# A decoder trunk on one core: the row scale moved behind the projections, gated attention in 128-row matmuls, and the first up-projection sums on VectorE

## The chip, the cores and the metric

The kernel runs on one core of a Trainium2 chip. The metric is the device time of one execution in microseconds, the median of several; lower is better. A core has five engines with queues of their own: PE (TensorE, matmuls and transposes; its weight loads are shown apart as PEld), DVE (VectorE), ACT (ScalarE), POOL (GpSimd) and SP (SyncE, here the queue that issues most transfers). Each engine works off its instructions in order and waits on semaphores of the others. Matmul results go to eight banks of PSUM.

## The reference, cut to what matters

One decoder layer on x of 1024 rows by 1024 columns, in float32:

```python
h = x * rsqrt(mean(x*x, -1) + 1e-6) * mix_norm
z = h @ w_in        # columns: gq 256, gk 256, gv 512, gr 512, glr 16, sq 512, sk 128, sv 128
log_a = log_sigmoid(glr @ w_alpha2 + b_alpha) / 16
o_gla = silu(gr) * rms_norm(gated_linear_attention(gq / 8, gk, gv, log_a))    # 4 heads of 64 / 128
o_swa = sliding_window_attention(rms_norm(sq), rms_norm(sk), sv, sinks)       # 8 heads of 64, window 128
x = x + concat([o_gla, o_swa]) @ w_out
u = causal_depthwise_conv3(rms_norm(x) @ w_up)      # 1024 -> 2 x 2816
a, b = split(u)
out = x + (silu(a) * b) @ w_down
```

## The kernel before, in words

Rows are worked in eight tiles of 128 (t = 0 to 7). A product that has to be near float32 is made of three fast passes: `split` (L90) stores an operand as a rounded part `hi` (a cast on ACT) and a remainder `lo` (a subtraction on POOL or DVE), and PE multiplies hi x hi, hi x lo and lo x hi. So one tile's projection of 1024 to 512 columns is 24 matmuls of 128x512 (`dense`, L279; `unit_q_part`, L643, for the first ones, named `dq`). The transposed, split rows are kept in `big`, the split weights in `qw`, `kw`, `vw`, `gw`, `rw` and `wow` by stage. Matmuls on plain float32 operands (the gated attention's and the small ones) aren't split.

The stages follow each other: the query projection `dq` with the first norm, the K and gate projection `dk`, the V projection `dv`, then `dg` (gated attention's q and k) and `dr` (its output gate) with both attentions between, the output projection `do` (two halves of columns), and the FFN, whose up and down products are made with seven instead of eight block products (operands such as A11, A12, S1 to S4 are blocks of w_up or sums of them). Before the first norm's transposes, `norm1_stat` squares a row tile on ACT, turns the sum into 1/sqrt on DVE and POOL (`rms_scale`, L156), and multiplies x by that and by `mix_norm` on DVE. `mix_norm` is spread over the partitions by a matmul with one row of ones (`mix`, L1003). Then PE transposes the tile (`n1pt`, L238), ACT and DVE split it into `big`. The x tiles take turns in three buffers.

In the sliding-window part K's tile and the 16 gate columns are transposed (`kpt`), and the gate's 17 rows (16 and one of ones) times `wa` give `za` (L368). In the gated part each tile has scores `ga` (L532, with 64 of the 128 partitions per head), `go` (L543, scores times values, and L546, queries times the running state `s_mid`) and the state's increment `cs` (L508).

The code lists steps with times in units of a tile (`at`), is sorted by them, and the framework's scheduler then sets each engine's order by a simulated timeline, so that instructions of several steps mix. Around the output projection the steps `up_operand` (L719) and `first_sums` (L713) prepare the first weights of the FFN: splits on ACT and POOL, sums on POOL. At the same time `norm2_stat` and `norm2_rows` (L183, L190) do the second norm: squares on ACT, `n2v` on DVE, the power `n2r` on POOL, two products `n2h` on DVE, and the transposes `n2pt` on PE. The last step, `last_row` (L973), makes eight row tiles of the last two chunks; each half of a tile is added on DVE and sent out by SP.

Of the kernel before, what the change touches and what calls it, by code (L numbers as in the profile page):

```python
# [9 lines left out]
F32 = mybir.dt.float32  # L10
# [7 lines left out]
P = 128  # L18
T = 1024
D = 1024  # L20
# [14 lines left out]
def hymba_layer_kernel(ctx, tc, x, mix_norm, w_in, w_alpha2, b_alpha, gla_norm,  # L35
# [31 lines left out]
    RAW_BUFS, K4, K2 = 3, 6, 4  # L67
# [51 lines left out]

    for h in range(8):  # L120
# [28 lines left out]

    def load_x(t, parts=1):  # L150
# [13 lines left out]

    def norm1_stat(t):
        xt = xts[t]
        junk = px.tile([P, D], F32, tag="junk", name=f"junk_{t}", bufs=1)
        ss = px.tile([P, 2], F32, tag="n1ss", name=f"n1ss_{t}", bufs=2)
        if t == 0:
            act.activation(junk[:, 0:512], xt[:, 0:512], AF.Square, accum_out=ss[:, 0:1])  # L170
            dve.tensor_tensor_reduce(junk[:, 512:], xt[:, 512:], xt[:, 512:], 1.0, ss[:, 0:1],
                                     ALU.mult, ALU.add, ss[:, 1:2])
        else:
            act.activation(junk, xt, AF.Square, accum_out=ss[:, 1:2])
        r = rms_scale(ss[:, 1:2], D, 1, f"n1{t}", px, "n1")
        for i, c in enumerate(halves):
            dve.scalar_tensor_tensor(xt[:, c], xt[:, c], r[:, 0:1], mixn[:, c] if t > 1 else mix_ps[i],
                                     op0=ALU.mult, op1=ALU.mult)

    def norm1_tr(t):  # L180
        norm_tr(t, xts.pop(t), "n1")
# [50 lines left out]

    def norm_tr(t, h, tag):
        for q in range(2):
            pt = bank(f"{tag}pt_{t}_{q}")
            for k in range(4):
                c = (q * 4 + k) * P
                pe.transpose(pt[:, k * P:(k + 1) * P], h[:, c:c + P], ident)  # L238
            ptv = pt.rearrange("p (k c) -> p k c", k=4)
            hi, lo = big[:, t, q * 4:q * 4 + 4, 0, :], big[:, t, q * 4:q * 4 + 4, 1, :]  # L240
            act.copy(hi, ptv)
            dve.tensor_sub(lo, ptv, hi.bitcast(F32))
# [10 lines left out]
    def raw_dma(name, c0, n, k2):  # L253
# [3 lines left out]
        if name == "k":  # L257
            sp.dma_start(rv[:, :, 0:256], rows[:, :, CSK:CSK + 256])
            sp.dma_start(rv[:, :, 256:272], rows[:, :, CG:CG + 16])
        else:  # L260
            sp.dma_start(rv, rows[:, :, c0:c0 + n])

# [35 lines left out]
    wa = gl.tile([17, 256], F32, name="wa")  # L298
    glan = gl.tile([P, 1], F32, name="glan")

    def load_small():
# [6 lines left out]
        sp.dma_start(wa[16:17, :], b_alpha)  # L308
        dve.tensor_mul(sinks_s, sinkb, islope)
# [5 lines left out]
    def head_rms(ps_ap, nh, name):  # L315
        sq = k2_tile(name + "sq")
        act.activation(sq[:, :nh * HD], ps_ap, AF.Square)
# [5 lines left out]
    def q_post(t, pb):  # L323
        r = head_rms(pb, 8, f"q{t}")
        rs = gl.tile([P, 8], F32, tag="rs", name=f"rs{t}", bufs=2)
        dve.tensor_mul(rs, r, qscale)
# [8 lines left out]
    def kvl_post(t, pb):  # L335
        r = head_rms(pb[:, 0:P], 2, f"k{t}")
        act.copy(vv[:, t, :], pb[:, P:2 * P])
        gn = gl.tile([P, 17], F32, tag="gn", name=f"gn{t}", bufs=4)
        pool.memset(gn[:, 16:17], 1.0)
        dve.tensor_copy(gn[:, 0:16], pb[:, 256:272])  # L340
# [7 lines left out]
    def kvl_tr(t):  # L348
# [12 lines left out]
        gt = gl.tile([17, P], F32, tag="gt", name=f"gt{t}", bufs=1)  # L361
        act.copy(gt, pt[0:17, P:2 * P])
# [86 lines left out]

    state = gl.tile([P, 2, P], F32, name="state")  # L450
    s_mid = [gl.tile([P, 2, 256], F32, name=f"s_mid{i}") for i in range(2)]
    asb = [gl.tile([P, 2, 256], F32, name="asb0")]
    for s in s_mid + asb:
        pool.memset(s, 0.0)
# [29 lines left out]
    def gla_qk(t, pb):  # L484
# [3 lines left out]
        dve.scalar_tensor_tensor(qk[:, 0:256], pb[:, 0:256], 0.125, ex[:, 0], op0=ALU.mult, op1=ALU.mult)  # L488
        dve.tensor_mul(qk[:, 256:512], pb[:, 256:512], ex[:, 1])
        if t < NT - 1:  # L490
            dve.tensor_mul(kd, pb[:, 256:512], ex[:, 2])
        gqk[t] = qk

    def gla_tr(t):
# [4 lines left out]
        qt = k2_tile(f"gqt{t}").rearrange("p (i c) -> p i c", i=4)  # L499
        act.copy(qt, pb.rearrange("p (i c) -> p i c", i=4))  # L500
        gqt[t] = qt
# [16 lines left out]
    def gla_mid(t):  # L518
        dc, sm = gdec[t], s_mid[t % 2]
        for h in range(4):  # L520
            pr, lo = h // 2, h % 2
            r = HALF[lo]
            act.activation(sm[r, pr, lo * P:(lo + 1) * P], state[r, pr], AF.Copy,
                           scale=dc[r, pr * 2:pr * 2 + 1])

    def gla_a(t):
        qt = gqt[t]
        for lo in range(2):
            pb = bank(f"ga{t}_{lo}")
            r = slice(lo * 64, (lo + 1) * 64)  # L530
            for pr in range(2):
                pe.matmul(pb[:, pr * P:(pr + 1) * P], lhsT=qt[r, 2 + pr, :], rhs=qt[r, pr, :],  # L532
                          start=True, stop=True)
            dve.copy_predicated(asb[0][:, lo].rearrange("p (q c) -> p q c", q=2),
                                amask.rearrange("p (q c) -> p q c", q=1).broadcast_to((P, 2, P)),
                                pb[:, 0:256].rearrange("p (q c) -> p q c", q=2))
# [667 lines left out]
```

## Time and profile before

| | us |
|---|---|
| median of 3 runs (1075.02 to 1076.96) | 1076.39 |
| profiled execution, its time | 1077.87 |
| its span, first to last instruction | 1075.9 |
| PE busy | 1063.8 |
| DVE / POOL / ACT busy | 780.6 / 635.4 / 493.8 |

The span is what the profiler saw from the first instruction to the last; some 2 us of the execution's time lie around it. PE is nearly always busy, so the place to look for time is where it isn't, or where a matmul costs more than its like. In the rows of the timeline the first number is the start, the second the length of the group, then engine, line, operation, written tile <- read tiles, shape, and the count; in brackets how long the engine was idle ahead of it, and for whom it waited. In the rows by window the columns are PE, PEld, DVE, ACT and POOL busy with counts, the granted clock of PE, the share of the transfer engines and GB/s.

### The profile page before, as it was taken

The numbers are of one execution on the slowest core, as the hardware profiler recorded it, in microseconds if no ns is written. First come the engines' busy times: TensorE is split into PE (matmuls) and PEld (weight loads), VectorE is DVE, ScalarE is ACT, GpSimd is POOL, SyncE is SP. The second block draws the span as 40 slices with busy tenths as digits, with TensorE's granted clock in tenths as the row PEclk, the third lists the DMA queues.
The fourth block names the chain that finished last, engine by engine and source line by source line (L and its number), as shares of the span: only waits on it lengthen the run. The fifth ranks groups of instructions, "written<-read, shape, count | busy, mean of one in ns | idle before, by whom it ended". The sixth has DMA issues, their size and how long they took to land.

```text
span 1075.9 us, 13898 instructions
## 1 busy us (share of the span) xinstructions
PE 1063.8 (99%) x4976; PEld 855.9 (80%) x4976; DVE 780.6 (73%) x1287; ACT 493.8 (46%) x998; POOL 635.4 (59%) x509
## 2 busy tenths in 40 slices
PE   7999999999999999999999999999999999999998
PEld 5898778777788878888888888888888888888886
DVE  6665546555222279788988979797979799897976
ACT  5326646546331235554444444444444445444441
POOL 4392224234552323866878787777868697877750
PEclk9999999999999999999999999999999999999999
DMA  6142113102007201221111121212121211111104
GB/s 210 58 142 67 32 31 98 33 8 65 15 24 251 59 1 39 59 59 46 53 41 59 59 59 42 77 40 79 39 61 38 59 40 59 59 59 59 40 19 157
DMA packets 67342, 67.13 MB, mean 62 GB/s; under 512 B 4616, under 2 KB 51913, under 8 KB 67274
## 3 DMA queue, kind: packets, MB, share of 16 engines
q1 hardware_dynamic: 63432, 61.53, 18.5%
q10 hardware_dynamic: 3842, 4.73, 1.9%
q8 instruction: 39, 0.64, 0.3%
q14 instruction: 29, 0.24, 0.1%
HBM read 57.33 MB, written 4.19 MB: 57 GB/s over the span
## 4 chain that ended last, share of the span: by engine, by line
PE 97%; DMA 1%; DVE 1%; POOL 0%; ACT 0%; issue 0%; SPq 0%; DVEq 0%; ACTq 0%
PE fb L775 38%; PE dn_P L956 18%; PE do L283 7%; PE dg L283 4%; PE dv L283 4%; PE dr L283 4%; PE dq L283 3%; PE dk L283 2%; PE gb L775 2%; PE pv L444 1%; PE ppt L432 1%; PE dq L649 1%; PE fb L983 1%; PE dl L983 1%; PE sc L400 1%; PE ga L532 1%
## 5 line engine op out<-in xcount | busy, mean ns | idle before, releaser
L960 DVE TENSOR_TENSOR acc<-acc,dn_P 128x1024 f32<-128x1024 f32 x140 | 169.8, 1214 | 65.7 <-PE dn_P L956 65.5
L956 PE MATMUL dn_P<-dw,dg 128*128 128x512 f32 x840 | 215.8, 392 | 0.0
L956 PEld LDWEIGHTS dn_P<-dw,dg 128*128 128x128 f32 x840 | 157.7, 188 | 37.1
L283 PE MATMUL do<-wow,big 128*128 128x512 f32 x384 | 94.5, 403 | 0.0
L283 PEld LDWEIGHTS do<-wow,big 128*128 128x128 f32 x384 | 72.3, 191 | 16.7
L95 POOL TENSOR_TENSOR dw<-dn,dw 128x512 fp32r<-128x512 f32 x50 | 69.6, 1392 | 25.2 <-PE dn_P L956 22.3
L827 ACT COPY ca<-fb 128x512 f32<-128x512 f32 x62 | 36.3, 585 | 72.6 <-PE fb L775 72.5
L421 POOL TENSOR_TENSOR pr<-pr,sm 128x1024 f32<-128x1024 f32 (+1 forms) x16 | 28.6, 1787 | 63.9 <-DVE sm L419 45.6
L775 PE MATMUL fb<-big,S1w 128*128 128x512 f32 x252 | 63.1, 396 | 0.0
L775 PE MATMUL fb<-big,S4w 128*128 128x512 f32 x252 | 62.9, 396 | 0.0
L775 PE MATMUL fb<-big,A11w 128*128 128x512 f32 x252 | 62.9, 396 | 0.0
L775 PE MATMUL fb<-ex,S2w 128*128 128x512 f32 x252 | 62.8, 397 | 0.0
L775 PE MATMUL fb<-ex,S3w 128*128 128x512 f32 x252 | 62.8, 396 | 0.0
L775 PE MATMUL fb<-big,A12w 128*128 128x512 f32 x252 | 62.6, 396 | 0.0
L782 DVE SCALAR_TENSOR_TENSOR ua<-fb,cc,ua 128x511 f32<-128x511 f32 x84 | 62.1, 740 | 0.5 <-ACT ua L787 0.3
L775 PE MATMUL fb<-ex,A22w 128*128 128x512 f32 x252 | 62.5, 397 | 0.0
L775 PEld LDWEIGHTS fb<-big,S1w 128*128 128x128 f32 x252 | 47.4, 188 | 11.6
L775 PEld LDWEIGHTS fb<-big,A11w 128*128 128x128 f32 x252 | 47.4, 188 | 11.6
L775 PEld LDWEIGHTS fb<-big,S4w 128*128 128x128 f32 x252 | 47.4, 188 | 11.6
L775 PEld LDWEIGHTS fb<-ex,S2w 128*128 128x128 f32 x252 | 47.4, 188 | 11.4
L775 PEld LDWEIGHTS fb<-ex,A22w 128*128 128x128 f32 x252 | 47.4, 188 | 11.4
L775 PEld LDWEIGHTS fb<-ex,S3w 128*128 128x128 f32 x252 | 47.4, 188 | 11.4
(433 smaller groups left out, 2439.4 us busy)
## 6 DMA issues: line engine op xcount, KB each, us to landing
up<-in_w_up_dram SPq DMA_DIRECT2D x44, 512.0 KB, 3.8
dn<-in_w_down_dram SPq DMA_DIRECT2D x22, 512.0 KB, 3.5
acc<-in_x_dram SPq DMA_DIRECT2D x8, 512.0 KB, 7.1
out_dram<-acc SPq DMA_DIRECT2D x16, 256.0 KB, 2.0
xt<-in_x_dram SPq DMA_DIRECT2D x7, 512.0 KB, 4.1
qraw<-in_w_in_dram SPq DMA_DIRECT2D x4, 512.0 KB, 7.1
vraw<-in_w_in_dram SPq DMA_DIRECT2D x4, 512.0 KB, 4.5
graw<-in_w_in_dram SPq DMA_DIRECT2D x4, 512.0 KB, 3.6
```

The costliest lines, as they stand in the source:

```text
L95: (eng or pool).tensor_sub(lo, src, hi.bitcast(F32))
L283: pe.matmul(pb[:, :n], lhsT=big[:, t, k, ra, :], rhs=ws[k][:, rb, :n], start=(k == 0 and i == 0), stop=(k == KD - 1 and i == 2))
L400: pe.matmul(pbs[-1][:, j % 2, :], lhsT=q[:, g, qc], rhs=kt[:, g, kc], start=True, stop=False)
L421: pool.tensor_tensor(pr[:, :, s0:], pr[:, :, s0:], den[:, hs].rearrange("p (j o) -> p j o", o=1).broadcast_to((P, 4, n)), ALU.mult)
L432: pe.transpose(pb[:, j * P:(j + 1) * P], pr[:, j, b * P:(b + 1) * P], ident)
L444: pe.matmul(pb[g * 64:(g + 1) * 64, :], lhsT=vv[:, t - 1 + b, g * 64:(g + 1) * 64], rhs=pts[t, g][:, b, :], start=(b == b0), stop=(b == 1))
L775: pe.matmul(pb, lhsT=w[:, ra, k, :], rhs=b_operand(bn, k, rb), start=(onto is None and i == 0), stop=(i == 11), skip_group_check=onto is n ...
L782: dve.scalar_tensor_tensor(dst, src, w, dst, op0=ALU.mult, op1=ALU.add)
L827: act.copy(dst, pb)
L956: pe.matmul(pb[:, i], lhsT=g[:, ra, c:c + P], rhs=w[:, rb, :], start=(onto is None and n == 0), stop=(n == 2), skip_group_check=onto is no ...
L960: dve.tensor_add(acc, acc, pb)
L983: pe.matmul(pb, lhsT=g[:, ra, (t % 4) * P:(t % 4 + 1) * P], rhs=w[:, rb, :], start=(ch == NCH - 2 and i == 0), stop=(ch == NCH - 1 and i = ...
```

## The change

The row scale 1/sqrt is no longer multiplied into x. x times `mix_norm` is transposed and split, and the scale (`rn`, computed beside it) is applied to what comes out of each projection: as the scale operand of ACT's copies, squares and SiLU, and in DVE's products. x's fourth tile has a buffer of its own, its load follows the third's, and half of the first weight piece is loaded from ACT's queue. `mix_norm` is spread by split matmuls of 128 rows, and PE gets ten matmuls of ones (`warm`) at the start. The first part, up to the third query tile, is written out in an order (`FIRST`) that is fixed for each engine (`pin`).

In the gated attention the query blocks of two heads stand in a block-diagonal tile `qbd` (zeros elsewhere), so that scores take two matmuls of 128 rows and 256 columns instead of four of 64 rows and 128 columns, and the state's product takes four of 128 columns instead of two of 256. The gate's product `za` has 128 rows, of which 111 are zero.

The first sums of the FFN, and the remainders of A11 and A12 of its first two chunks, go from POOL to DVE, and two of these steps are kept behind a mark in each engine's order (`behind`). In the last row tile the second half is made and sent in two quarters.

```diff
-        r = rms_scale(ss[:, 1:2], D, 1, f"n1{t}", px, "n1")
-        for i, c in enumerate(halves):
-            dve.scalar_tensor_tensor(xt[:, c], xt[:, c], r[:, 0:1], mixn[:, c] if t > 1 else mix_ps[i],
-                                     op0=ALU.mult, op1=ALU.mult)
+    def norm1_mul(t, i):
+        if i == 0:
+            xts["h", t] = px.tile([P, D], F32, tag="h1", name=f"h1_{t}", bufs=1)
+        c = halves[i]
+        dve.tensor_mul(xts["h", t][:, c], xts[t][:, c], mixn[:, c] if t > 3 else mix_ps[i])
...
+        act.activation(xt, xt, AF.Square, accum_out=ss)
+        dve.tensor_scalar(ss, ss, 1.0 / D, EPS, op0=ALU.mult, op1=ALU.add)
+        pool.tensor_tensor(rn[:, 0, t:t + 1], ss, mhalf[:, 0:1], ALU.pow)
+        dve.tensor_scalar(rn[:, 1, t:t + 1], rn[:, 0, t:t + 1], 0.125, None, op0=ALU.mult)
...
-        xt = xts[t] = px.tile([P, D], F32, tag="xt", name=f"xt_{t}", bufs=3)
+        xt = xts[t] = k4_tile("xt_3") if t == 3 else px.tile([P, D], F32, tag="xt", name=f"xt_{t}", bufs=3)
...
+        elif (name, k2) == ("q", 0):
+            act.dma_start(rv[:, 0], rows[:, 0, c0:c0 + n])
+            sp.dma_start(rv[:, 1], rows[:, 1, c0:c0 + n])
...
-        act.activation(sq[:, :nh * HD], ps_ap, AF.Square)
+        act.activation(sq[:, :nh * HD], ps_ap, AF.Square, scale=row_scale(t))
...
-        gt = gl.tile([17, P], F32, tag="gt", name=f"gt{t}", bufs=1)
-        act.copy(gt, pt[0:17, P:2 * P])
+        gt = gl.tile([P, P], F32, tag="gt", name=f"gt{t}", bufs=2)
+        pool.memset(gt, 0.0)
+        act.copy(gt[0:17], pt[0:17, P:2 * P])
...
-        qt = k2_tile(f"gqt{t}").rearrange("p (i c) -> p i c", i=4)
-        act.copy(qt, pb.rearrange("p (i c) -> p i c", i=4))
+        for lo in range(2):
+            act.copy(qbd[t % 2][HALF[lo], :, lo, :], pv[HALF[lo], 0:2])
+        kt = k2_tile(f"gkt{t}")[:, 0:256].rearrange("p (i c) -> p i c", i=2)
+        act.copy(kt, pv[:, 2:4])
...
-        for lo in range(2):
-            pb = bank(f"ga{t}_{lo}")
-            r = slice(lo * 64, (lo + 1) * 64)
-            for pr in range(2):
-                pe.matmul(pb[:, pr * P:(pr + 1) * P], lhsT=qt[r, 2 + pr, :], rhs=qt[r, pr, :],
-                          start=True, stop=True)
+        pb = bank(f"ga{t}")
+        for pr in range(2):
+            pe.matmul(pb[:, pr * 256:(pr + 1) * 256], lhsT=gqt[t][:, pr, :], rhs=qbd[t % 2][:, pr],
+                      start=(pr == 0), stop=(pr == 1))
...
-        for pr in range(2 if t else 0):
-            pe.matmul(pb[:, pr * 256:(pr + 1) * 256], lhsT=qt[:, pr, :], rhs=s_mid[t % 2][:, pr, :],
-                      start=False, stop=(pr == 1))
+        for h in range(4 if t else 0):
+            pe.matmul(pb[:, h * P:(h + 1) * P], lhsT=qbd[t % 2][:, h // 2, h % 2, :], rhs=s_mid[t % 2][:, h // 2, :],
+                      start=False, stop=(h == 3))
...
-        act.copy(vg[0][:, t, :], dense(t, blocks["v"], 512, f"dv{t}"))
+        act.activation(vg[0][:, t, :], dense(t, blocks["v"], 512, f"dv{t}"), AF.Copy, scale=row_scale(t))
...
-        sums(s1, ra[:, 0:4], rb[:, 0:4], rb[:, 4:8])
-        pool.tensor_sub(ra[:, 4:8], ra[:, 4:8], ra[:, 0:4])
+        sums(s1, ra[:, 0:4], rb[:, 0:4], rb[:, 4:8], dve)
+        dve.tensor_sub(ra[:, 4:8], ra[:, 4:8], ra[:, 0:4])
...
-        split(src, w[:, 0], w[:, 1])
+        split(src, w[:, 0], w[:, 1], dve if ch < 2 and name[1] == "1" and name[0] == "A" else None)
...
+            for c0, c1 in ((0, 256), (256, 512)) if (t, hf) == (NT - 1, 1) else ((0, 512),):
...
+    def warm_up(n):
+        for i in range(n):
+            pe.matmul(warm_bank, lhsT=ones_r, rhs=warm, start=True, stop=True)
...
+    FIRST = ((norm1_mul, 0, 0), (q_hi, 0), (q_lo, 0, pool), (norm1_mul, 0, 1), (q_hi, 1), (warm_up, 2), (norm1_tr, 0, 0),
...
+    for f, *a in FIRST:
+        f(*a)
+    pin()
```

PE's first instructions before: `mix` spreads the norm weight, `n1pt` are the transposes of row tiles 0 and 1, `dq` the query projection of tile 0.

```order
L1003 MATMUL mix_146<-mix_row,ones 128x512
L1003 MATMUL mix_148<-mix_row,ones 128x512
L238 MATMUL n1pt_0_178<-ident,xt_143 128x128 x4
L238 MATMUL n1pt_1_185<-ident,xt_143 128x128 x4
L649 MATMUL dq_198<-qw_172,big 128x512 x3
L649 MATMUL dq_198<-qw_175,big 128x512 x3
L649 MATMUL dq_198<-qw_192,big 128x512
L238 MATMUL n1pt_0_220<-ident,xt_152 128x128 x4
L649 MATMUL dq_198<-qw_192,big 128x512 x2
```

And now, after five warm-up matmuls (`warm`) and the first `mix`:

```order
L1074 MATMUL mix_187<-mix_149,ones_r 128x512
L1074 MATMUL mix_192<-mix_148,ones_r 128x512
L1074 MATMUL mix_192<-mix_149,ones_r 128x512
L1066 MATMUL warm<-warm,ones_r 128x512 x2
L254 MATMUL n1pt_0_205<-ident,h_0_195 128x128 x4
L1066 MATMUL warm<-warm,ones_r 128x512
L254 MATMUL n1pt_1_214<-ident,h_0_195 128x128 x4
L688 MATMUL dq_222<-qw_197,big 128x512 x3
L688 MATMUL dq_222<-qw_201,big 128x512 x3
L688 MATMUL dq_222<-qw_229,big 128x512 x3
L254 MATMUL n1pt_0_240<-ident,h_1_234 128x128 x4
```

Warm-up matmuls stand ahead of and between the first steps, and the transposes of tile 1 come behind three whole groups of `dq`.

POOL at the start of the second half of the output projection, before: `wow` are the remainders of the last output weights, `up` and `s` the FFN's first weights and their sums, `n20r` the power of the second norm's row tile 0.

```order
L95 TENSOR_TENSOR wow_6_3624<-wo_3_3621,wow_6_3624 128x512
L95 TENSOR_TENSOR A11w_3819<-up_0_3630,A11w_3819 128x512
L95 TENSOR_TENSOR A12w_3935<-up_0_3630,A12w_3935 128x512
L709 TENSOR_TENSOR s_0_3433<-up_1_3632 128x512
L95 TENSOR_TENSOR A11w_3938<-up_0_3669,A11w_3938 128x512
L95 TENSOR_TENSOR A12w_3941<-up_0_3669,A12w_3941 128x512
L710 TENSOR_TENSOR up_1_3632<-up_0_3630,up_1_3632 128x512
L160 TENSOR_TENSOR n20r<-n20v,mhalf 128x1
L711 TENSOR_TENSOR up_0_3630<-s_0_3433,up_0_3630 128x512
```

DVE at the same place now (on POOL the row of `n20r` follows the last `wow` directly):

```order
L95 TENSOR_TENSOR A11w_3838<-up_0_3649,A11w_3838 128x512
L95 TENSOR_TENSOR A12w_3954<-up_0_3649,A12w_3954 128x512
L715 TENSOR_TENSOR acc<-acc,do_0_3653 128x512
L165 TENSOR_SCALAR n20v<-n2ss_3680 128x1
L208 SCALAR_TENSOR_TENSOR n2h_3679<-acc,n20r,ffn 128x512 x2
L95 TENSOR_TENSOR A11w_3957<-up_0_3688,A11w_3957 128x512
L749 TENSOR_TENSOR s_0_3452<-up_1_3651 128x512
L95 TENSOR_TENSOR A12w_3960<-up_0_3688,A12w_3960 128x512
L715 TENSOR_TENSOR acc<-acc,do_4_3690 128x512
L750 TENSOR_TENSOR up_1_3651<-up_0_3649,up_1_3651 128x512
L260 TENSOR_TENSOR big<-n2pt_0_3725,big 128x4x128
L751 TENSOR_TENSOR up_0_3649<-s_0_3452,up_0_3649 128x512
```

The eight moved rows stand on DVE between the second norm's products, three of them behind `n20v` and ahead of row tile 4's sum.

More of the change, by code (lines that the diff above doesn't have):

```diff
@@ L450, in hymba_layer_kernel @@
     state = gl.tile([P, 2, P], F32, name="state")
-    s_mid = [gl.tile([P, 2, 256], F32, name=f"s_mid{i}") for i in range(2)]
-    asb = [gl.tile([P, 2, 256], F32, name="asb0")]
-    for s in s_mid + asb:
+    s_mid = [gl.tile([P, 2, P], F32, name=f"s_mid{i}") for i in range(2)]
+    qbd = [gl.tile([P, 2, 2, P], F32, name=f"qbd{i}") for i in range(2)]
+    asb = gl.tile([P, 4, P], F32, name="asb")
+    for s in qbd + [asb]:
         pool.memset(s, 0.0)
@@ L1055, in hymba_layer_kernel @@
             at(u + SUMS, norm2_sums, t)
-    at(-8.06, load_small)
     at(5.3, const_a)
@@ L1088, in hymba_layer_kernel, with mark, behind @@
         at(TR + t + 1.3, lambda tt=t: gate_tr(tt, psb.pop(("r", tt))))
+    ahead = {}
+    def mark():
+        ahead.update((ins.engine, ins.name) for ins in nc.cur_bb.bb.instructions)
+    def behind(f, *a):
+        n = len(nc.cur_bb.bb.instructions)
+        f(*a)
+        for ins in nc.cur_bb.bb.instructions[n:]:
+            if ins.engine in ahead:
+                tc.add_manual_dep(ins, ahead[ins.engine], mybir.DependencyInfo(
+                    mybir.DependencyClass.NoSync, mybir.DependencyReason.DATA), reason="order of the program")
+    at(TO + 8.006, mark)
     at(TO - 0.05, open_acc)
```

210 lines of the change are left out of this document (118 added, 92 removed).

## The prediction

> **What bounds the kernel now.** I read the page's busy table, then PE's waits, then PE's rows in order of time at the three places where PE isn't dense, then the last wait.
>
> ```profile
> span 1075.9 us, 13898 instructions
> PE 1063.8 (99%) x4976; PEld 855.9 (80%) x4976; DVE 780.6 (73%) x1287; ACT 493.8 (46%) x998; POOL 635.4 (59%) x509
> PE n1pt L238 <- DVE n11v L158: 2.5, 1, 2.5
> PE n2pt L238 <- DVE n2h L193: 2.2, 1, 2.2
> ```
>
> PE is busy 1063.8 of 1075.9 us and waits only at the start and once in the middle. So the time falls only by what PE no longer waits for, by cheaper matmuls, and by what stands after the last one; other engines matter where they hold PE up. The profiled execution took 1077.87 us (1.97 around its span), 1.48 above the median of 1076.39; I work out differences on it and subtract them from the median.
>
> **The start.**
>
> ```profile
> 3.11 3.75 PE L1003 MATMUL mix<-mix_row,ones 1*128 1x512 f32 x4 [3.11 <-DMA mix_row<-in_mix_norm_dram]
> 7.11 1.11 PE L238 MATMUL n1pt<-ident,xt 128*128 128x128 f32 x4 [0.25 <-DVE xt L177]
> 7.54 1.14 ACT L92 CAST qw<-qraw 128x512 fp32r<-128x512 f32 x2 [3.15 <-DMA qraw<-in_w_in_dram]
> 8.23 1.27 POOL L95 TENSOR_TENSOR qw<-qraw,qw 128x512 fp32r<-128x512 f32 x1 [1.96 <-ACT qw L92]
> 9.13 1.06 ACT L174 ACTIVATE junk<-xt 128x1024 f32<-128x1024 f32 x1 [0.46 <-DMA xt<-in_x_dram]
> 11.53 3.33 PE L649 MATMUL dq<-qw,big 128*128 128x512 f32 x7
> 11.91 0.58 ACT L241 CAST big<-n1pt 128x512 fp32r<-128x512 f32 x1
> 13.37 0.68 DVE L242 TENSOR_TENSOR big<-n1pt,big 128x512 fp32r<-128x512 f32 x1
> 14.66 1.05 PE L238 MATMUL n1pt<-ident,xt 128*128 128x128 f32 x4
> 16.46 0.60 PE L238 MATMUL n1pt<-ident,xt 128*128 128x128 f32 x4
> 16.81 7.94 PE L649 MATMUL dq<-qw,big 128*128 128x512 f32 x33
> 24.59 1.04 PE L238 MATMUL n1pt<-ident,xt 128*128 128x128 f32 x8
> 25.38 1.42 PE L649 MATMUL dq<-qw,big 128*128 128x512 f32 x5
> ```
>
> A row's own length ends late; the next start is the cost. 33 matmuls from 16.81 to 24.59 are 236 ns each, 8 transposes to 25.38 are 99 ns each; but the 7 matmuls from 11.53 to 14.66 are 447 ns each. So PE runs at half speed there, though the granted clock reads 1.00 in that stretch. When it becomes dense, at 16.81, PE has done 10 matmuls (2.36) and 16 transposes (1.58): it stands as if dense since 12.87.
>
> The Trainium skill (TensorE: Matmul & The Clock Gate, Part 1) says that the array starts at half clock and gets the full one after a window of about 3.4 us of sustained work. The spacing of these matmuls agrees with it.
>
> In the change the row scale leaves this path: x times the norm weight goes straight into the transposes, and warm-up matmuls run as soon as two memsets are done, which I put at about 2 us, so I take 236 ns for the first matmuls. Then the weights' arrival orders the front. The first two pieces land at 7.54 as now (same bytes ahead of them); ACT casts them and both halves of row 0 (two at 0.57, two at 0.58) until 9.84, then the third piece (its block, now third in the queue, lands at 9.13, as the third transfer does now) until 10.41; POOL's remainder takes 1.27, 11.68; PE's third group ends 12.15; row 1's transposes 0.40, ACT's cast 0.58, DVE's remainder 0.68: 13.8; then 7 matmuls to 15.5, where the second half of row 1 is ready. By then 21 matmuls (4.96) and 12 transposes (1.19) are done: as if dense since 9.35. That is 3.5 earlier. With one tile for h, row 2's remainder comes behind row 3's products on DVE, for which I give back 0.1: **-3.4**. Bounds: -1.0, if all 21 run at 447 (4.4 more, of which about 2 falls into waits for weights), and -5.3, where only the 7.54 landing bounds it (dense from 7.54). I take the middle, as the chain's rows give it. The fourth x tile's load and half of the first weights on ACT's queue move issues only; what SP now reaches later (small vectors, K weights) isn't needed before the K stage, some 40 us on. The scale comes back as an operand of ACT's and DVE's later instructions, some 0.1 us each on engines that PE outlasts there; squares of x only move. All 0, hidden by PE's 5.6 us per block; uncovered it would be some 4 us of ACT over the stage.
>
> **The small matmuls.**
>
> ```profile
> 123.42 0.69 PE L368 MATMUL za<-wa,gt 17*128 17x256 f32 x2
> 124.05 1.43 PE L283 MATMUL dv<-vw,big 128*128 128x512 f32 x5
> 125.41 0.44 PE L691 MATMUL pcc<-ident,cr 44*128 44x44 f32 x4
> 201.20 0.71 PE L532 MATMUL ga<-gqt 64*128 64x128 f32 x4
> 201.84 0.66 PE L432 MATMUL ppt<-ident,pr 128*128 128x128 f32 x4
> 213.17 1.06 PE L543 MATMUL go<-vg,asb 128*128 128x128 f32 x8
> 214.06 1.03 PE L546 MATMUL go<-s_mid,gqt 128*128 128x256 f32 x4
> 215.02 0.71 PE L532 MATMUL ga<-gqt 64*128 64x128 f32 x4
> 256.57 0.72 PE L532 MATMUL ga<-gqt 64*128 64x128 f32 x8
> 257.23 3.07 PE L283 MATMUL dg<-gw,big 128*128 128x512 f32 x12
> ```
>
> A `za` of 17 rows costs 0.63, and the 5 matmuls behind it 1.36, 0.18 above 5 x 236. With 128 rows it is half of the L546 pair (0.96 for two of 256 columns): 0.48. 8 x (0.15 + 0.18) = -2.6 at best, 8 x 0.15 = -1.2 if the step behind stays: **-1.3**. The scores `ga` of a block were two pieces of 0.64 in five blocks and one of 0.66 where both stand together (three blocks): 8.4. As two 128-row matmuls of 256 columns they cost an L546 pair, 0.96, so 7.7; five entries fewer at about 0.12 (half the step measured behind za, rounded up): **-1.3**. Bounds +1.0 (below) and -2.9. The state part of `go`, L546, 0.96, becomes four of 128 columns, which L543 gives as 0.89: 0. ACT's extra copies and DVE's one wide predicated copy lie under the 5.6 us of projection that the order keeps between.
>
> The Trainium skill (the same page, Why this matters for your kernels) says that a matmul with 32 rows takes as long as one with 128, and that the gain of small ones is that different row groups run together. By that padding za brings 0 and joined halves lose: a rival below.
>
> **The gap at 378.75.**
>
> ```profile
> 375.79 2.96 PE L283 MATMUL do<-wow,big 128*128 128x512 f32 x12
> 376.22 0.15 DVE L158 TENSOR_SCALAR n20v<-n2ss 128x1 f32<-128x1 f32 x1 [2.35 <-ACT n2h L187]
> 377.20 1.30 POOL L710 TENSOR_TENSOR up<-up,up 128x512 f32<-128x512 f32 x1
> 378.45 0.56 POOL L160 TENSOR_TENSOR n20r<-n20v,mhalf 128x1 f32<-128x1 f32 x1
> 379.05 3.42 DVE L193 SCALAR_TENSOR_TENSOR n2h<-acc,n20r,ffn 128x512 f32<-128x512 f32 x2 [2.67 <-POOL n20r L160]
> 380.94 0.78 PE L238 MATMUL n2pt<-ident,n2h 128*128 128x128 f32 x4 [2.19 <-DVE n2h L193]
> 381.37 5.03 PE L283 MATMUL do<-wow,big 128*128 128x512 f32 x14
> 386.23 0.60 PE L238 MATMUL n2pt<-ident,n2h 128*128 128x128 f32 x4
> 382.00:384.00 2.00, 2.00 (x6) 1.59 (x5) 1.67 (x3) 1.24 (x2) 0.00 (x0) 0.50 0.00 0
> 385.00:390.00 5.00, 5.00 (x27) 4.08 (x27) 2.80 (x4) 0.95 (x2) 0.07 (x1) 1.00 0.00 0
> 400.00:405.00 5.00, 5.00 (x26) 4.04 (x25) 4.89 (x10) 2.51 (x5) 0.40 (x1) 1.00 0.02 3
> ```
>
> PE waits 2.19 us for row 0 of the second norm, and then runs at a granted clock of 0.50: 14 matmuls in 4.86 instead of 3.30, 1.56 lost. The norm's power stands on POOL behind remainders and sums of the first up weights; 376.37 to 378.45 is that queue, and DVE's two products take 3.42, where two like the sum of row L242 would take 1.4, while POOL works beside them. With those eight on DVE, and the statistic ahead of chunk 1's casts on ACT, the power starts at about 376 (or sooner), and DVE's first half ends by 377.5, before PE asks at 378.75: -3.75. Late next is block 4's norm: DVE owes five of the moved eight (0.68 each, 3.4) ahead of it; between 385 and 390 DVE is busy 2.80 of 5, so it has about that much room. By the rows it ends within 0.3 of PE's arrival at 385: **-3.6**. Bounds -3.75 and -0.5 (3.3 given back).
>
> **The end.**
>
> ```profile
> 1072.08 0.69 DVE L986 TENSOR_TENSOR acc<-acc,dl 128x512 f32<-128x512 f32 x1 [0.67 <-PE dl L983]
> DMA to landing us min/median/max: 2.0/2.0/2.1
> ```
>
> Behind the last matmul stand a sum of 0.69 and a transfer of 2.0. In two halves the last sum is 0.3 shorter, the transfer of half the bytes perhaps 0.3; twelve narrower matmuls add 0.1 of issue: **-0.5**, between 0 (all of 2.0 is latency) and -0.8.
>
> **Sum.** -3.4 - 1.3 - 1.3 - 3.6 - 0.5 = -10.1: 1067.8 on the profiled execution, 1066.3 on the median.
>
> **Rivals.**
> (1) The warm-ups don't open the clock, since PE waits between them: the start gains 1.0 and not 3.4, 1068.7. For: four us of `mix` matmuls ahead of 7.11 left it slow (4 transposes until 8.2). Against: the warm-ups and mix together fill some 5 us.
> (2) DVE takes POOL's place in the norm, and half of the gap comes back: 1068.1. For: it is busy 4.89 of 5 us from 400 on; against: its idle 2.2 us from 385 on.
> (3) Rows don't matter: za 0, and the three joined blocks go from 0.66 to 0.96 with no entries saved, +1.0: 1066.3 + 1.3 + 2.3 = 1069.9. Against: za's 0.63 beside the 0.48 of a full pair's half.
> (4) More than summed, the front limited by the first landing and every step behind small matmuls gone: 1066.3 - 1.9 - 1.3 - 1.0 = 1062.1.
> (5) Slower: the pinned order makes the front a chain of waits on casts, so that the half clock outlasts it through the query blocks. A matmul then costs 211 ns more; it needs 10.1 / 0.211 = 48 such beyond the 21 to undo all gains, and 60, with 2.5 over, to measure as slower: 1078.9. Against: dense from 15.5 on by the rows.
>
> **The numbers.** Forecast 0.60, (1) 0.13, (2) 0.11, (3) 0.08, (4) 0.05, (5) 0.03. The range takes in (1) to (3) and most of the way to (4), 1062.0 to 1071.0; beyond lie (5) and several together. A difference of 0.2%, 2.2 us, is about what can be told from none: faster 0.95, same 0.02, slower 0.03.
>
> **What would show it.** The first query matmuls at about 236 ns and before 10 us; the K stage starting 3.4 earlier; no PE wait near 378 and a granted clock of 1.00 there; za near 0.48 and no more than 0.1 behind it; 1.0 per `ga`; under 2.7 us from the last matmul to the last landing. Wrong would be: 447 ns in the front, a PE wait on n2h in 380 to 425, or a new wait on ACT or DVE in the attention stages.

## The result, and the profile after

The changed kernel takes 1065.62 us (median of 4 runs, 1065.32 to 1066.28). The kernel before took 1075.70 on the same chip (4 runs, 1074.57 to 1076.96). The ratio is 0.9907 with a 95% interval of 0.989 to 0.9924. The forecast was 1066.3 in a range of 1062 to 1071; it was taken off a median of 1076.39, from the first three runs of the kernel before. So the time came out 0.7 from the forecast; whether the terms behind it hold is what the rest asks.

The page of the profiled run of the changed kernel (1065.66 us) begins so; the two lines under it are PE's waits (us in total, times, longest):

```profile
span 1063.9 us, 13937 instructions
PE 1057.7 (99%) x4988; PEld 857.0 (81%) x4988; DVE 788.4 (74%) x1306; ACT 495.2 (47%) x1002; POOL 629.1 (59%) x511
PE dq L688 <- POOL qw L296: 0.5, 1, 0.5
PE gb L815 <- ACT big L256: 0.2, 1, 0.2
```

The waits of 2.5 us (`n1pt`) and 2.2 us (`n2pt`) are gone. Nothing of their size took their place: the largest wait behind the first query matmul is 0.5.

The start, by PE's timeline (start, length, engine, line, instruction, number; in brackets the idle time ahead of it and what ended it), and then two weight loads from the same view at its finest:

```profile
1.66 2.50 PE L1066 MATMUL warm<-warm,ones_r 128*128 128x512 f32 x5 [1.66 <-DVE warm L123]
6.71 0.60 PE L254 MATMUL n1pt<-ident,h 128*128 128x128 f32 x4
8.28 2.00 PE L688 MATMUL dq<-qw,big 128*128 128x512 f32 x7
10.75 0.73 PE L688 MATMUL dq<-qw,big 128*128 128x512 f32 x2 [0.47 <-POOL qw L296]
11.67 3.55 PE L688 MATMUL dq<-qw,big 128*128 128x512 f32 x12
15.42 5.14 PE L688 MATMUL dq<-qw,big 128*128 128x512 f32 x21
...
5.52 0.33 PEld L1074 LDWEIGHTS mix<-mix,ones_r 128*128 128x128 f32 x1
6.25 0.19 PEld L1066 LDWEIGHTS warm<-warm,ones_r 128*128 128x128 f32 x1
```

The query matmuls start at 8.28 in place of 11.53 and run at full speed. The 12 from 11.67 take 3.39 to the next row at 15.06, or 0.28 each; from 15.42 they are dense. The length of these weight loads tells the clock: 0.33 at half speed, 0.19 at full. It changes at about 6.1 here. In the kernel before it changed at about 16.0.

The middle, PE, then GpSimd and VectorE, and the row of the view by stretches (its third number from the end is the granted clock):

```profile
370.85 0.60 PE L254 MATMUL n2pt<-ident,n2h 128*128 128x128 f32 x4
371.20 2.59 PE L318 MATMUL do<-wow,big 128*128 128x512 f32 x10
367.74 0.56 POOL L167 TENSOR_TENSOR n20r<-n20v,mhalf 128x1 f32<-128x1 f32 x1 [7.39 <-DVE n20v L165]
368.34 1.42 DVE L208 SCALAR_TENSOR_TENSOR n2h<-acc,n20r,ffn 128x512 f32<-128x512 f32 x2 [0.74 <-POOL n20r L167]
372.00:374.00 2.00, 2.00 (x13) 1.62 (x11) 2.00 (x6) 1.22 (x3) 0.00 (x0) 1.00 0.00 0
```

GpSimd was idle for 7.39 us when the power came, VectorE's products take 1.42 and not 3.42, and row 0 of the second norm is ready before PE asks. The clock stays at 1.00.

The end: the last six matmuls and the last sum. From its end to the end of the span are 3.05 us.

```profile
1059.56 0.87 PE L1025 MATMUL fb<-dnw,g 128*128 128x256 f32 x6
1060.47 0.42 DVE L1028 TENSOR_TENSOR acc<-acc,fb 128x256 f32<-128x256 f32 x1
```

The next table says where the time went. It gives the first start of a tile's matmuls on PE's timeline, in us, before and after, and what the stage in front of that point gained.

| point | before | after | stage in front of it | gained | forecast |
|---|---|---|---|---|---|
| first `dk` (key stage) | 64.67 | 61.09 | start and queries | 3.58 | 3.4 |
| first `dg` | 168.69 | 162.09 | keys and values, with the eight `za` | 3.02 | 1.3 |
| first `do` | 321.71 | 313.98 | gated attention, with `ga` | 1.13 | 1.3 |
| first `gb` | 422.65 | 410.97 | output projection, with the gap | 3.95 | 3.6 |
| end of span | 1075.87 | 1063.94 | FFN and end | 0.25 | 0.5 |

These two profiled runs are 11.9 us apart, 1.8 more than the sum forecast, and 1.7 of that is `za`. The medians are 10.1 apart: the profiled run of before (1077.87) was one of its slower ones. Why there are such is told below.

### The profile page after: what moved, and what is told of

The parts are those of the page before. It is cut to its first block, busy times and chain, and to the rows that moved or that the text cites. A ratio compares the mean times of both kernels' runs of the same rounds, so it can differ in the third digit from the quotient of the medians.

```text
span 1063.9 us, 13937 instructions
## 1 busy us (share of the span) xinstructions
PE 1057.7 (99%) x4988; PEld 857.0 (81%) x4988; DVE 788.4 (74%) x1306; ACT 495.2 (47%) x1002; POOL 629.1 (59%) x511
## 4 chain that ended last, share of the span: by engine, by line
PE 99%; DMA 1%; POOL 0%; SPq 0%; ACT 0%; DVE 0%; issue 0%
PE fb L815 39%; PE dn_P L996 18%; PE do L318 8%; PE dg L318 4%; PE dr L318 4%; PE dv L318 4%; PE dq L318 3%; PE dk L318 2%; PE gb L815 2%; PE dq L688 2%; PE pv L487 2%; PE ppt L475 1%; PE dl L1025 1%; PE fb L1025 1%; PE sc L443 1%; PE go L582 1%
```

## The experiments

All are edits of the changed kernel unless the text says otherwise. Its median of 1065.62 and the stages of the table are what they are held against. One more number helps with the start: from the first query matmul to the first `dk` took 52.81 us in the profiled run of the changed kernel, but 52.58 to 52.60 in seven of the kernels below that have the same start, so 52.60 is used. (PE's wait for the third weight piece is 0.47 in that one profile and 0.26 to 0.28 in the seven.)

**The start without warm-ups.** (In the code cuts, `...` stands for what is left out.)

```
-    RAW_BUFS, K4, K2, N_WARM = 3, 6, 4, 5
+    RAW_BUFS, K4, K2, N_WARM = 3, 6, 4, 0
-  ... (warm_up, 2), (norm1_tr, 0, 0), ... (warm_up, 1), (norm1_tr, 0, 1), (warm_up, 2), ...
+  ... (norm1_tr, 0, 0), ... (norm1_tr, 0, 1), ...
```

> The changed kernel without its ten warm-up matmuls, all else in the same order. Theory (the warm-ups open the clock, the row scale's way out gives the rest): the first query matmuls fall back from about 236 ns to about 447 ns until some 21 of them are done, the key stage starts 1.0 to 2.4 us later than the 61.09 us of the changed kernel, and the time is 1066.6 to 1068.0 against 1065.6. Rival (warm-ups do nothing, mix matmuls and transposes open the clock alone): the spacing stays near 236 ns, the key stage within 0.2 us of 61.09, 1065.6. Second rival (the warm-ups hold the transposes up): the first query matmul starts before 8.28 and the time falls by up to 0.5.

It took 1066.05 us (1065.83 to 1066.18): 0.43 more. From the first query matmul to `dk` are 53.07 us, 0.47 more. PE's timeline, and the weight loads that bracket the change of speed:

```profile
4.90 1.65 PE L1074 MATMUL mix<-mix,ones_r 128*128 128x512 f32 x3 [0.34 <-DVE mix L95]
6.57 1.94 PE L254 MATMUL n1pt<-ident,h 128*128 128x128 f32 x8
8.33 2.39 PE L688 MATMUL dq<-qw,big 128*128 128x512 f32 x7
11.06 0.73 PE L688 MATMUL dq<-qw,big 128*128 128x512 f32 x2 [0.34 <-POOL qw L296]
...
8.49 0.34 PEld L688 LDWEIGHTS dq<-qw,big 128*128 128x128 f32 x1
9.65 0.19 PEld L688 LDWEIGHTS dq<-qw,big 128*128 128x128 f32 x1
```

The clock opens here without any warm-up, at about 9.4 us; in the ten profiles with warm-ups it opens between 4.7 and 7.1. Only two or three query matmuls run at half speed, and the seventh starts 2.00 behind the first in place of 1.60. The wait for the third weight piece takes none of that back: it is 0.34 here. Theory and rival both missed: not the 1.0 to 2.4 us of a clock that stays shut over 21 matmuls, and not 0 either.

**The row scale back on the path, warm-ups kept.**

```
+        if t < 2:
+            dve.scalar_tensor_tensor(xts["h", t][:, c], xts[t][:, c], row_scale(t), mix_ps[i], ...)
...
-    FIRST = ((norm1_mul, 0, 0), ... (q_hi, 1), (warm_up, 2), ...
+    FIRST = ((norm1_stat, 0), (norm1_mul, 0, 0), ... (q_hi, 1), (norm1_stat, 1), (warm_up, 2), ...
```

> The changed kernel with its warm-ups, but rows 0 and 1 of x multiplied by their row scale ahead of the transposes again, so that their sum of squares, the power on GpSimd and the product stand on the path (these two blocks are scaled twice, which alters their values only). Theory (both parts are needed): the first query matmul starts 2 to 3.3 us later than 8.28, the key stage 2.0 to 3.6 us later than 61.09, and the time is 1067.6 to 1069.2. Rival (the clock alone brings the gain of the start): key stage within 1.0 of 61.09, time below 1066.6. If the clock closes again while PE waits for the scale, the query matmuls show 447 ns in place of 236.

The sum of squares of row 0 is shared here by ScalarE and VectorE. It took 1068.89 us (1068.51 to 1069.91): 3.3 more. In the profiled run `dk` starts at 65.38, 4.3 later, where the kernel before had 64.67. PE's timeline and one row of the view by stretches:

```profile
7.97 0.63 PE L263 MATMUL n1pt<-ident,h 128*128 128x128 f32 x4 [1.35 <-DVE h L178]
11.21 0.72 PE L697 MATMUL dq<-qw,big 128*128 128x512 f32 x2 [1.47 <-ACT big L265]
12.35 3.35 PE L697 MATMUL dq<-qw,big 128*128 128x512 f32 x7 [0.41 <-DVE big L269]
16.00 3.55 PE L697 MATMUL dq<-qw,big 128*128 128x512 f32 x12
13.00:14.00 1.00, 1.00 (x4) 0.81 (x3) 1.00 (x2) 0.00 (x0) 1.00 (x1) 0.50 0.47 103
```

The first query matmul is 2.9 late. The clock had been opened, but PE then waits 1.47 and 0.41, and from 12.4 to 15.8 the granted clock is 0.50: seven matmuls take 3.15 to the transposes at 15.50, or 450 ns each. That stretch isn't typical: the profiled run is the longest of the five (1069.91) and the only one that lists a mean clock of 0.998; the others list 1.000, which leaves no room for such a stretch behind the clock's opening, and took 1068.51 to 1068.94. So 3.3, and not 4.3, is the price of the row scale on the path, most of it the 2.9 by which the first query matmul is late. Taken together, the two experiments say that the row scale's way off the path brings nearly all of the start's gain. The warm-ups bring 0.4 of it, and by themselves they didn't hold the clock open in the profiled run. The rest of the new start (the fixed order, the fourth x buffer, the halved first weight load, the 128-row `mix`) was not undone piece by piece; with the scale on the path 3.3 of the 3.6 us are lost, so it gains little by itself.

**`za` with 17 and with 100 rows.** Only the number of rows that the eight products read is changed; every instruction stays in its place.

```
-        pe.matmul(pt[:, 0:256], lhsT=gt, rhs=wa, start=True, stop=True)
+        pe.matmul(pt[:, 0:256], lhsT=gt[0:17], rhs=wa[0:17], start=True, stop=True)     # the other: 0:100
```

> The changed kernel with only the eight za matmuls back to 17 rows; buffers, memsets and the order on every engine stay. Theory (a step where a matmul of few rows stands between 128-row ones, paid by it and by the one behind it): za goes from 0.32 us to 0.63 us in the mean, and with the step behind it the eight cost 1.3 to 2.6 us: 1066.9 to 1068.2 against 1065.6. Rival (rows don't matter, 17 rows take as long as 128): 0, 1065.6, za stays at 0.32.

> The changed kernel with the eight za matmuls on 100 rows; order and all else stay. Theory a (the step belongs to a change of the array's row split, which 100 rows, more than 64, don't make): as with 128 rows, za 0.32 us, 1065.6. Theory b (every matmul of fewer than 128 rows pays it): as with 17 rows, za about 0.63 us and 1066.9 to 1068.2. Rival (rows don't matter at all): 0 here and with 17 rows.

With 17 rows: 1068.18 us (1067.99 to 1068.41), 2.56 more. With 100: 1065.84 (1065.28 to 1065.98), the same as with 128. From `dk` to `dg` it is 103.96 us with 17 rows, 101.01 with 100, 101.00 with 128: 2.95 for eight, 0.37 each. The weight loads about the same `za` show how, first with 17 rows, then with 100:

```profile
83.92 0.19 PEld L444 LDWEIGHTS sc<-kt,ql 128*128 128x128 f32 x1
84.24 0.29 PEld L411 LDWEIGHTS za<-wa,gt 17*128 17x128 f32 x2
84.87 0.19 PEld L443 LDWEIGHTS sc<-kt,qt 128*128 128x128 f32 x1 [0.33 <-issue]
```

```profile
84.26 0.19 PEld L444 LDWEIGHTS sc<-kt,ql 128*128 128x128 f32 x1
84.38 0.31 PEld L411 LDWEIGHTS za<-wa,gt 100*128 100x128 f32 x2
84.72 0.19 PEld L443 LDWEIGHTS sc<-kt,qt 128*128 128x128 f32 x1
```

With 100 rows a load starts 0.12 after the one ahead, beside the matmul that still runs, and the next full load follows 0.34 after the first of `za`. With 17 rows these are 0.32 and 0.63, and the load engine stands idle ahead of the full load. So the 17-row load isn't started beside the full matmul ahead of it, nor the next full load beside the 17-row matmul. By the starts of PE's matmuls at this `za`, 0.09 of the loss lies ahead of it, 0.10 between its two passes and 0.20 behind it: it is paid on both sides. The Trainium skill (TensorE: Matmul & The Clock Gate, Why this matters for your kernels) has a single matmul of 32 rows take as long as one of 128. In this stream of 128-row matmuls the 17 rows cost 0.37 us more, and the measurement decides.

**The gated attention's scores and tiles as before.** (`s_mid`, `gla_tr`, `gla_mid`, `gla_a` and `gla_o` of the kernel before.)

```
+        for lo in range(2):
+            pb = bank(f"ga{t}_{lo}")
+            r = slice(lo * 64, (lo + 1) * 64)
+            for pr in range(2):
+                pe.matmul(pb[:, pr * P:(pr + 1) * P], lhsT=qt[r, 2 + pr, :], rhs=qt[r, pr, :],
+                          start=True, stop=True)
```

> The changed kernel with the gated attention's scores, q and k tiles and state products as they were before (scores of 64 rows, one head half per bank). Theory (a step at each switch to 64-row matmuls and back): the stage from the first dg to the first dr, 96.56 us in the changed kernel and 98.64 before, grows by 1.3 to 2.9, 2.1 by the difference of the two; the time is 1066.9 to 1068.5, 1067.7 taken, against 1065.6. Rival (rows don't matter, two joined half-row matmuls are cheaper than one of 128 rows and 256 columns): the time falls by 1.0 to 1064.6. Second rival (ACT's extra copies in the changed form cost PE time): it falls too, and PE shows a wait on ACT in the changed kernel that is gone here.

It took 1066.59 us (1066.43 to 1067.42), 0.97 more, a little below the range given. From `dg` to `dr` the stage grows by 2.05, as expected. But from `dr` to `do` it is 54.37 and not 55.33: 0.96 shorter. The two stages share a border that the order of the last blocks moves, so only their sum counts, 152.98 against 151.89: 1.09. No wait of PE comes or goes. The rival with a gain is out. By the starts of PE's matmuls the scores alone fall by 2.4, from 8.33 to 5.90, and other small matmuls between `dg` and `do`, `pv` above all, give 1.3 of it back; why these do was not tried. The edit takes back the rows, the tiles and the state products at once, so the 1.1 isn't the price of 64 rows alone.

**The gap, four ways.** Two things were changed there: the engine of eight sums and remainders (VectorE for GpSimd) and the order (`behind`: first sums and chunk 1's operands behind the work on the second norm's first row). The experiments take one, the other, and both away:

```
-        sums(s1, ra[:, 0:4], rb[:, 0:4], rb[:, 4:8], dve)             # engine back: e4_gap_pool, e4c_gap_undone
+        sums(s1, ra[:, 0:4], rb[:, 0:4], rb[:, 4:8])
...
-        split(src, w[:, 0], w[:, 1], dve if ch < 2 and ... else None)
+        split(src, w[:, 0], w[:, 1])
...
-    at_us(-12, behind, first_sums)                                     # order back: e4b_no_behind, e4c_gap_undone
+    at_us(-12, first_sums)
```

> The changed kernel with the first up weights' sums and the remainders of A11 and A12 back on GpSimd; the added order (behind) stays. Theory (the power of the second norm waits in GpSimd's queue, PE waits for it and then runs at half clock): PE waits 1 to 2.2 us for n2h near 368 to 371, the granted clock is 0.50 for some 3.4 us behind it, and the time is 1067.5 to 1069.4, 1069.2 taken (+3.6). Rival (the order alone, which puts these operations behind the norm's, brings the gain): no wait on n2h, within 0.4 of 1065.6. Third possibility: a wait without the half clock, +1 to +2.2.

> The changed kernel without the added order (behind): the eight sums and remainders of the first up weights stay on VectorE, but all eight, and the four casts that feed them on ScalarE, now stand ahead of the second norm's first row on their engines. The run with these operations on GpSimd and the order kept took 1065.9, so the theory is now: what counts is what stands ahead of the norm, not the engine. Theory: eight operations of 0.68 us ahead of it make the row late, PE waits 1 to 3 us for n2h, and a stretch at half clock of up to 1.6 follows: 1066.6 to 1070.2, 1068.5 taken. Rival (the engine counts: VectorE is fast enough in any order): no wait, 1065.6 to 1065.9.

> The changed kernel with the gap's part undone as a whole: sums and remainders on GpSimd and no added order, so that the power of the norm stands behind six of them in GpSimd's queue as before. Theory (the order alone brings the gain): the wait of 2.2 us on n2h and the half clock behind it are back, from the first do to the first gb 100.9 in place of 97.0, time 1069.2 to 1069.6. Rival (the wait before the change came from something else, such as the later start of the stage): under 0.5 more than 1065.6.

| | VectorE | GpSimd |
|---|---|---|
| with the order | 1065.62, PE waits 0 | 1065.91, PE waits 0 |
| without it | 1067.69, PE waits 1.4 | 1068.20, PE waits 2.2 |

My theory for the engine alone failed by its whole size: +3.6 expected, 0.3 measured, and from `do` to `gb` the profiles have 97.01 against 96.99, so nothing in this stage. GpSimd and VectorE in that run:

```profile
367.97 0.56 POOL L167 TENSOR_TENSOR n20r<-n20v,mhalf 128x1 f32<-128x1 f32 x1 [2.90 <-DVE n20v L165]
368.50 1.28 POOL L749 TENSOR_TENSOR s<-up 128x512 f32<-128x512 f32 x1
368.56 3.47 DVE L208 SCALAR_TENSOR_TENSOR n2h<-acc,n20r,ffn 128x512 f32<-128x512 f32 x2 [0.74 <-POOL n20r L167]
371.08 0.60 PE L254 MATMUL n2pt<-ident,n2h 128*128 128x128 f32 x4
```

The power goes ahead of the sums, because the order says so, and GpSimd is free when it comes. VectorE's two products take 3.47 beside GpSimd's work, as in the kernel before, and even so the first of them ends before 371.08. With the order gone and the eight on VectorE, the reason for the wait is another, as VectorE's and ScalarE's rows show:

```profile
367.44 0.69 DVE L757 TENSOR_TENSOR up<-up 128x512 f32<-128x512 f32 x1
368.04 0.68 DVE L715 TENSOR_TENSOR acc<-acc,do 128x512 f32<-128x512 f32 x1
368.81 1.06 ACT L202 ACTIVATE n2h<-acc 128x1024 f32<-128x1024 f32 x1 [2.10 <-DVE acc L715]
```

The sum that finishes row 0 (`acc`) stands behind the eight, at 368.04, where the changed kernel has it at 365.46. ScalarE's statistic waits 2.10 for it. From `do` to `gb` are 98.53 us, 1.54 more. With both undone the old picture is back, by GpSimd's and PE's rows and a stretch, but for one thing:

```profile
369.38 1.29 POOL L750 TENSOR_TENSOR up<-up,up 128x512 f32<-128x512 f32 x1
370.62 0.56 POOL L167 TENSOR_TENSOR n20r<-n20v,mhalf 128x1 f32<-128x1 f32 x1
373.10 0.63 PE L254 MATMUL n2pt<-ident,n2h 128*128 128x128 f32 x4 [2.16 <-DVE n2h L208]
373.49 3.50 PE L318 MATMUL do<-wow,big 128*128 128x512 f32 x14
374.00:376.00 2.00, 2.00 (x10) 1.60 (x9) 1.85 (x3) 1.08 (x2) 0.10 (x1) 1.00 0.00 0
```

PE waits the same 2.2 us, and the 14 matmuls behind it take 3.34 to the next row at 376.83, not 4.86: the clock stays at 1.00. From `do` to `gb` are 99.37 us, 2.38 above the changed kernel, where 100.9 was expected. The wait doesn't always close the clock.

The same part alone, put into the kernel before:

```
+        eng.tensor_add(s1, a21, a22)
+        eng.tensor_sub(a21, a11, a21)
+        eng.tensor_sub(a11, s1, a11)
...
+    at_us(-12, behind, first_sums)
```

> The kernel before with only the gap's part of the change: the first up weights' sums and the remainders of A11 and A12 on VectorE, and the added order. Theory (the parts add up): 3.6 us less than before, 1072.1 to 1073.1 against 1075.7 to 1076.7; no wait on n2h; from the first do to the first gb 97.0 in place of 100.94. Rival (VectorE takes GpSimd's place): half of it, 1.8 less. Rival (the parts need each other, since the start's pinned order moves what stands here): less than 0.5.

It took 1073.93 us (8 runs, 1072.88 to 1074.46), against 1076.69 for the kernel before (20 runs, ratio 0.9974, 0.9964 to 0.9985): 2.8 less. From `do` to `gb` are 97.03 us, in place of 100.94. So in the profiled runs the part brings 3.9, in the medians 2.8: the stage is as expected, the time 0.8 above the range given. The parts add up; the medians differ from the profiles for the reason that comes next.

**The kernel before, once more.** Nothing is edited.

> The kernel before once more, unchanged, for a second profile: its runs spread over 3.6 us (1074.2 to 1077.8), those of the changed kernel over 1.0. Theory a (the spread is in the start, where transfers and the clock's opening meet): the first dk moves by 1 us or more against 64.67. Theory b (it is in the middle: the length of the wait on n2h and of the half clock behind it): from the first do to the first gb differs by 0.5 or more from 100.94, dk stays within 0.5. Theory c: both within 0.3, and the spread lies outside what these two stages show.

The profiled run took 1078.59. `dk` starts at 65.45, 0.78 later than in the first profile, and from `do` to `gb` are 100.93, 0.01 less. In the middle:

```profile
381.70 0.76 PE L238 MATMUL n2pt<-ident,n2h 128*128 128x128 f32 x4 [2.18 <-DVE n2h L193]
382.11 5.04 PE L283 MATMUL do<-wow,big 128*128 128x512 f32 x14
```

So the start moves, and the half clock is here again. None of the three theories passes its own test: 0.78 is under the 1 of theory a and over the 0.3 of theory c, and 0.01 is far from the 0.5 of theory b. Two profiles are too few for it. But each run also lists the mean granted clock, and one stretch of 3.4 us at half clock makes it 0.998. Of 50 runs of the kernel before, 33 list 0.998 and took 1077.5 in the mean, and 17 list 0.999 or 1.000 and took 1075.4. The run with both parts of the gap undone has one of five at 0.998, and it is the slowest (1069.19; the three at 1.000 took 1068.01 to 1068.20). So 2.1 of the 5.0 us between the shortest and the longest of the 50 go with whether the clock closed. That it closed at this wait is shown for the two profiled runs, both of the kind at 0.998, and inferred for the others. The rest, 2.5 to 2.9 us within each kind, isn't traced; the start's 0.78 is part of it.

**The last block in one piece.**

```
-            for c0, c1 in ((0, 256), (256, 512)) if (t, hf) == (NT - 1, 1) else ((0, 512),):
+            for c0, c1 in ((0, 512),):
```

> The changed kernel with the last block in one piece. Theory: from the last matmul's start to the end as before the change, 0.3 to 0.5 us more: 1065.9 to 1066.1. Rival (the 2.0 us of the last transfer don't depend on its size and twelve narrower matmuls cost as much as the shorter sum saves): within 0.1 of 1065.6, no later end of the span behind the last product pair.

It took 1065.67 us (1065.52 to 1066.49), which can't be told from 1065.62. By the trace, from the first `dl` to the end of the span are 28.16, and 27.88 in the changed kernel. Over all the profiles it is 28.11 to 28.16 in the four with the whole block and 27.87 to 28.06 in the nine with it halved at 256: about 0.2, below the theory's 0.3 to 0.5.

**A version beyond the change.**

```
-             ... (q_hi, 2), (q_lo, 2, pool), ...
+             ... (q_hi, 2), (q_lo, 2, dve), ...
-            for c0, c1 in ((0, 256), (256, 512)) if (t, hf) == (NT - 1, 1) else ((0, 512),):
+            for c0, c1 in ((0, 384), (384, 512)) if (t, hf) == (NT - 1, 1) else ((0, 512),):
```

> A version beyond the change: the third weight block's remainder on VectorE in place of GpSimd, which takes 0.69 us and not 1.28 and for which PE waited 0.5 us, and the last block cut at 384 in place of 256. Theory: the wait at 10.3 to 10.8 goes, the start gains 0.3 to 0.5; the last sum is 0.1 to 0.2 shorter: 1065.0 to 1065.3. Rival (VectorE then makes the product of row 1 late, which the transposes at 11.3 wait for): the wait moves on, 1065.6 to 1066.0.

It took 1065.44 us (1064.99 to 1065.93), 0.18 less, with ranges that overlap: unclear. PE's wait on `qw` is gone, and from the first query matmul to `dk` are 52.04 us, 0.56 less than 52.60. The other cut gives nothing: from the first `dl` to the end are 28.12, as with the whole block. The engine of the third remainder is worth keeping, if anything is.

## Why the prediction was right, point by point

- **Start, -3.4 forecast, -3.58 in the profiles.** The size and the chain of casts and remainders hold: the second half of row 1 was put at 15.5 and stands at 15.06. But what was credited with the clock is wrong. The step took 236 ns for the first matmuls on account of the warm-ups, and rival (1) priced them at 2.4. Without them the clock opens at 9.4 us all the same, and 0.4 is lost; that it opens there because PE no longer waits between 8.2 and 10.8 fits the trace, but nothing was changed to test it alone. The bound had 21 matmuls at half speed; there are two or three.
- **`za`, -1.3 forecast, -2.95 measured.** This is the term that was mis-sized. The forecast chose "8 x 0.15 = -1.2 if the step behind stays"; the best bound was -2.6. With 128 rows the step behind `za` goes too, and a third part goes that was not counted, some 0.09 each ahead of `za`.
- **`ga`, -1.3 forecast, -1.1 measured,** by the kernel with this part undone (0.97 in the medians). The sum is near, its parts are not: a block's scores cost 0.74 and not 0.96, and 1.3 comes back in matmuls that the forecast left alone. That these two errors nearly cancel is luck. The bound of -2.9 has no working in the prediction; rival (4) goes by -2.3. The state part was put at 0, and the trace has 6.29 for it after and 6.24 before.
- **Gap, -3.6 forecast, -3.95 in the profiles.** Size right, reason half wrong. The forecast had the power free "with those eight on DVE, and the statistic ahead of chunk 1's casts". The eight needn't move to VectorE: with them on GpSimd and the order kept, the stage is as long as in the changed kernel (97.01 and 96.99). Rival (2), VectorE as the new bound, doesn't happen: its 2.00 busy of 2.00 us behind 372 holds nobody up. And the 1.56 of half clock was booked as if each run paid it; by the listed clocks two runs in three do.
- **End, -0.5 forecast, -0.2 to -0.3 measured.** The shorter sum is there (0.42 for 0.69). Of the shorter transfer, for which the forecast had no row, little is seen: behind the last sum are 3.05 us after and 3.10 before, where the forecast counted the 2.0 of the transfer.
- **Sum.** The forecast's -10.1 met the medians' -10.1, and that close a hit is luck, for two errors offset each other: 1.7 too little for `za`, and 1.6 of half clock in the profiled run which the runs of the median have only in part. Rival (3) is out by the 17 and 100 rows, (4) came true for `za` alone, and (5) has no sign in the trace.

## What to carry to other kernels

A float32 matmul of 17 rows in a stream of 128-row ones pays on both sides; zeros up to 100 or 128 rows cost less here (0.37 us each). Numbers of rows between 17 and 100 were not measured by themselves. Where a small result waits in a queue behind bulk work, put it ahead in the order before you move the bulk to another engine: here the order brought the gain with either engine. A run's mean granted clock beside its time tells whether a wait cost only itself or closed the clock too, so look at it over many runs before one profiled run is taken as typical.

## What was not expected of the hardware

- Whether a wait of 2.2 us closes the clock changes from run to run of one kernel (by the listed clocks 33 of 50). In the two profiles of before, the clock opens at about 16.0 and 16.8 us, and the half clock begins at 381.3 and 382.1: 365.2 in both. With the row scale on the path it opens at 5.6 and closes at 12.4. Those are 107 and 2 stretches of 3.41 us, the length of the half clock in the profile of before (381.27 to 384.68). In all 14 profiles the clock also closes behind the last matmul, each time a whole number of such stretches behind an opening (310 in the changed kernel, from 6.09 to 1064.23). The Trainium skill (TensorE: Matmul & The Clock Gate, Part 1) says that activity is judged over a free-running window of about 3.4 us. The traces agree. By that grid the wait of before lies whole in one window, and in the kernel with the gap undone (open at 6.4, wait from 370.94 to 373.10) a border falls into it at 371.6, which leaves at most 1.5 us idle in one. That is worked out, and no run moved the wait against the grid on purpose.
- How much idle time in one window closes the clock can be read from the windows at hand: two with the row scale on the path, then two at the end of the kernel with the gap undone (the second number is PE's busy time, the third from the end the clock):

```profile
8.96:12.38 3.42, 1.54 (x8) 0.68 (x6) 0.99 (x4) 2.84 (x6) 0.69 (x2) 1.00 1.05 410
12.38:15.79 3.41, 3.41 (x9) 2.62 (x10) 2.21 (x3) 0.31 (x1) 1.66 (x1) 0.50 0.38 108
1061.09:1064.50 3.41, 1.69 (x11) 1.33 (x9) 1.46 (x3) 0.00 (x0) 0.00 (x0) 1.00 0.51 191
1064.50:1067.90 3.40, 0.00 (x0) 0.00 (x0) 0.00 (x0) 0.00 (x0) 0.00 (x0) 1.00 0.08 27
```

With PE busy for 1.54 us the next window ran at half clock, with 1.69 us it did not, and no window of the 14 profiles contradicts these two. PE's ends are modelled, so the limit is good to a tenth or so. An estimate from these numbers: if the windows start anywhere, a wait of 2.2 us closes the clock in 55 to 63 of 100 runs; 33 of 50 list it.
- The one-row `mix` matmuls of the kernel before kept PE busy for 3.75 us and did not open the clock. In its second profile they fill a whole window of the grid, from 3.19 to 6.60, and the transposes right behind still run at half speed, 0.21 us apart, where dense ones at full speed are 0.10 apart:

```profile
3.03 3.75 PE L1003 MATMUL mix<-mix_row,ones 1*128 1x512 f32 x4 [3.03 <-DMA mix_row<-in_mix_norm_dram]
7.19 1.12 PE L238 MATMUL n1pt<-ident,xt 128*128 128x128 f32 x4 [0.42 <-DVE xt L177]
```

So there it wasn't idle time that kept it shut. The 128-row matmuls of the changed kernel without warm-ups opened it within 4.5 us of 4.90. Whether the single row counts or that these `mix` matmuls are plain float32 was not tried.
